# Block sums of the resident operands made in pieces during the up products and kept in DRAM, instead of inside the refill

## The chip, the core and the metric

One core of a Trainium2 chip runs the whole kernel. The metric is the device time of one execution in microseconds; the time of a kernel is the median of several executions. A trace of one more execution was taken by the hardware profiler.

The engines by the profile's names: PE is TensorE (matmuls; PEld its weight loads), DVE is VectorE, ACT is ScalarE, POOL is GpSimd, SP is SyncE, which here only issues DMAs. Each engine works through its own instructions in order and waits on semaphores of the others. So does SP: a DMA whose buffer is not free yet holds up the DMAs behind it.

## The reference

One transformer layer with a mixer of two kinds of groups and a dense SwiGLU FFN, in float32. The change touches only the FFN:

```python
# x: (1, 2048, 1024); w_gate_up: (1024, 5632); w_down: (2816, 1024)
xn = rms_norm(x, ffn_norm_g[l])
gate, up = jnp.split(xn @ w_gate_up[l], 2, axis=-1)
x = x + (jax.nn.silu(gate) * up) @ w_down[l]
return rms_norm(x, final_norm_g)
```

## The kernel before

The attention, the gating and the output projection come first and end at about 1099 us of the trace; what follows is the FFN, and all of the change lies there.

**Products.** Each FFN matrix product is done on 2 x 2 blocks by a scheme with seven products instead of eight (Strassen's, in Winograd's form). One side, the resident operand, stays in SBUF for a whole *set* of work; the other side streams past it. The seven resident operands R0 to R6 come from the four blocks b11, b12, b21, b22 of the resident matrix: R0, R2 and R6 are b11, b21 and b22 as they are, R1, R3, R4 and R5 are sums, made by four adds, each of which builds on the one before: b12 = b22 - b12, b11 = b11 + b12, b21 = b21 - b11, b11 = b22 - b11. Every operand is then split into a high half in fp32r (a cast on ACT) and a low half (a subtraction on DVE), and a product is three matmuls a k-block: high x high, high x low, low x high.

**Sets, groups, rounds.** There are five sets: set 1 and set 2 are the up products (`Up`, 22 items each; the resident matrix is the transposed normed x, tensors XT[0] and XT[1] in DRAM), sets 3 to 5 are the down products (`Down`, 8 items each; the resident matrix is a part of w_down). The list `slots` runs over groups of two items and the seven products n = 0 to 6 of each. I call one n of one group a round: two items x 12 matmuls of 128x128 x 512 columns (9 in set 5). A group is 7 rounds, 168 matmuls (126 in set 5). Set 1 has 11 groups, 77 rounds.

**Streamed operands.** `load` fetches an item's rows (tile raw, or rawd for some down items) by DMAs on SP; `stream` makes its seven operands with four adds, two on POOL and two on DVE (`SE = 'pvpv'`, rows raw<-raw), and `split` gives each a wh (cast on ACT) and a wl (DVE). There are NW = 6 buffers each of wh and wl, and LW = 6 operands are made ahead, which is three rounds. raw has five buffers, so a load waits until an earlier item's split has let go of one.

**Results.** A product lands in one of six PSUM banks (tile pp) and is taken from there by ACT or DVE (`evac`: rows u, c, hT, xa, xb). In the order of the program the bank of a round is written again two rounds after that round at the earliest. The up products' hT is stored to DRAM (HD) and read back by the down products; the down products add to rows of x in the tiles xa, xb and, in the last set, sg.

**The refill, which the change edits.** `staged(s)` loads the four blocks of the next set's resident matrix into four tiles sg0 to sg3 of 128 x 2048 f32 (1 MB each; 128 x 1536 in set 5). The first add is put four rounds into the group ahead of a set's last one. In the last group of a set, `refill` makes the remaining adds and the seven splits (`keep`, `keep_as`), one operand a round, so that each R is replaced behind its last use. Table `TE` names the engine of each add: DVE, but POOL for the third add (b21 = b21 - b11) of set 5 and of set 1, which is never refilled. In the trace the adds are the rows sg<-sg,sg, and the splits' low halves the rows wl<-sg, wh<-sg, R1l, R3l, R4l<-sg (R0, R2, R5 and R6 live in tiles tagged wh and wl).

**What sets the order.** The functions write the work in program order; a scheduler then orders each engine's instructions, by priority and by when it takes operands and buffers to be ready. So an add can come earlier than the place at which it is written: the first add of set 3's sums stands in the first group of set 2.

Of the kernel before, what the change touches and what calls it, by code (L numbers as in the profile page):

```python
# [8 lines left out]
F32 = mybir.dt.float32  # L9
F32R = mybir.dt.float32r  # L10
AF = mybir.ActivationFunctionType
ALU = mybir.AluOpType
# [4 lines left out]
P = 128  # L17
S = 2048
D = 1024
# [6 lines left out]
CH = 512  # L26
# [25 lines left out]
KB = [8, 8, 6]  # L52
# [3 lines left out]
TE = ['vvvv', 'vvpv', 'vvvv', 'vvvv', 'vvvv', 'vvpv']  # L56
# [29 lines left out]
def trunk(ctx: ExitStack, tc: tile.TileContext, x, x_t, mix_g, w_in, b_f, ln_g, ln_b, w_st, b_st, on_g, w_out,  # L86
# [444 lines left out]
    for c in range(NCH):  # L531
# [4 lines left out]
        n = 0  # L536
# [761 lines left out]

    def staged(s):

        sg = stage()
        for i, t in enumerate(sg):
            if s < 3:
                ld(t, XT[s - 1][i])
                continue
            kh, r0 = KB[s - 3] // 2, sum(KB[: s - 3])
            r0 = (r0 + (i // 2) * kh) * P
            ld(t[:, 0:kh, :],
               w_down[r0 : r0 + kh * P, (i % 2) * CH : (i % 2 + 1) * CH].rearrange("(k p) n -> p k n", p=P))
        return sg  # L1310

# [7 lines left out]
    def tt(e, o, a, b, op):  # L1319
        (nc.vector if e == "v" else nc.gpsimd).tensor_tensor(o, a, b, op)  # L1320

    def keep_as(i, src, kh=4):
        rh, rl = resident(i)
        hi_of(nc.scalar, rh[:, 0:kh, :], src)
        lo_of(nc.vector, rl[:, 0:kh, :], src, rh[:, 0:kh, :])
        return rh, rl

    def refill(sg, kh, te):

        b11, b12, b21, b22 = (t[:, 0:kh, :] for t in sg)  # L1330

        def keep(i, src):
            return keep_as(i, src, kh)

        yield keep(0, b11)
        tt(te[1], b11, b11, b12, ALU.add)
        yield keep(1, b11)
        yield keep(2, b21)
        tt(te[2], b21, b21, b11, ALU.subtract)
        tt(te[3], b11, b22, b11, ALU.subtract)  # L1340
        yield keep(3, b11)
        yield keep(4, b12)
        yield keep(5, b21)
        yield keep(6, b22)
# [107 lines left out]
    class Down(Rows):  # L1452
# [15 lines left out]
        def source(self, t):  # L1468
            return XA[t]
# [131 lines left out]
    nextR = [None] * 7  # L1601
    for q in range(len(slots)):
# [7 lines left out]
        if n == 0 and i == 2 and s < 5:  # L1610
            sg = staged(s + 1)
        last = last and s < 5
        if n == 4 and s < 5 and i + 2 * len(its) == len(sets[s - 1]):
            b = [t[:, 0 : sets[s][0].kh, :] for t in sg]
            tt(TE[s + 1][0], b[1], b[3], b[1], ALU.subtract)
        if n == 0 and last:
            fill = refill(sg, sets[s][0].kh, TE[s + 1])
# [75 lines left out]
```

## Time and profile before

| | |
|---|---|
| median of 3 runs | 2384.66 us (2383.82 to 2389.83) |
| the profiled execution | 2382.4 us, span 2380.7 us |
| PE busy in the span | 2337.5 us (98%) |
| DVE, ACT, POOL busy | 1671.2 (70%), 1056.2 (44%), 633.6 us (27%) |
| granted TensorE clock, mean | 0.996 |
| first matmul of sets 1 to 5 | 1099.46, 1521.32, 1942.67, 2100.32, 2253.97 us |
| DMA over the span | 372.22 MB, mean 156 GB/s |

The span is what the profiler saw from the first to the last instruction; the execution's time has 1.7 us around it. A matmul of 512 columns has a row of about 0.39 us, but matmuls overlap in the pipeline; they start one every 0.227 us (38.08 us for the 168 of a group). Where a group takes longer, TensorE stood still or its clock was lower. A row of a list of groups reads: line, engine, operation, output<-inputs, shape, count | busy us, mean ns | idle time of the engine just before, and what ended it.

### The profile page before, as it was taken

To read this page: it belongs to the slowest core of one execution; us is meant where nothing else is said; L and a number is where in the kernel's file an instruction comes from. 1 tells how busy PE (TensorE), PEld (TensorE's weight loads), DVE (VectorE), ACT (ScalarE), POOL (GpSimd) and SP (SyncE) were. 2 spreads that over 40 slices of the span, in tenths; PEclk is the share of its full clock that TensorE was granted. 3 is DMA by queue.
4 is the path that set the end of the run, shared out by engine and by line. 5 is a ranking of instruction groups with operands and counts; after the bars stand their busy time and mean duration, and the time that the engine had idled before them with its cause. 6 is when DMAs were issued, how large, how long until landed. Compare 5 with 4: busy or idle time off the path is not lost. (4 is left out here: it accounts for less than half of the span.)

```text
span 2380.7 us, 31420 instructions
## 1 busy us (share of the span) xinstructions
PE 2337.5 (98%) x10582; PEld 1893.8 (80%) x10582; DVE 1671.2 (70%) x2736; ACT 1056.2 (44%) x1770; POOL 633.6 (27%) x705
## 2 busy tenths in 40 slices
PE   9999999999999989999999999999999999999997
PEld 7778777777777768878888888788888878888886
DVE  6658668888887676566655556965655596686888
ACT  5322137777778776344323233432323242332433
POOL 1100002122111232221323223332322245354531
PEclk9999999999999999999999999999999999999999
DMA  7845567666586664666232332433232345455453
GB/s 257 295 154 195 200 189 209 167 164 178 151 219 190 195 186 150 211 217 200 80 89 81 88 89 80 143 89 96 71 89 72 88 142 186 168 186 200 151 192 148
DMA packets 356425, 372.22 MB, mean 156 GB/s; under 512 B 22101, under 2 KB 275733, under 8 KB 354217
## 3 DMA queue, kind: packets, MB, share of 16 engines
q1 hardware_dynamic: 340280, 326.97, 45.3%
q0 software_dynamic: 7616, 27.33, 3.2%
q10 hardware_dynamic: 8368, 15.91, 1.8%
q8 instruction: 85, 1.39, 0.2%
q14 instruction: 76, 0.61, 0.1%
HBM read 249.15 MB, written 120.98 MB: 155 GB/s over the span
## 5 line engine op out<-in xcount | busy, mean ns | idle before, releaser
L128 ACT CAST wh<-raw 128x512 fp32r<-128x512 f32 (+2 forms) x492 | 301.9, 621 | 746.8 <-PE pp L1631 612.7
L131 DVE TENSOR_TENSOR wl<-raw,wh 128x512 fp32r<-128x512 f32 (+2 forms) x496 | 375.9, 767 | 81.5 <-ACT wh L128 81.0
L1631 PE MATMUL pp<-wl,wh 128*128 128x512 f32 x1056 | 325.3, 389 | 1.2 <-ACT u L1386 1.0
L1631 PE MATMUL pp<-wh,wh 128*128 128x512 f32 x1056 | 325.2, 389 | 0.0
L1320 POOL TENSOR_TENSOR raw<-raw 128x512 f32<-128x512 f32 (+1 forms) x124 | 171.2, 1382 | 518.3 <-DMA raw<-in_w_gu_dram 354.5
L131 DVE TENSOR_TENSOR Pl<-Pt,Ph 128x512 fp32r<-128x512 f32 (+1 forms) x320 | 195.6, 616 | 71.1 <-ACT Ph L128 69.8
L1631 PEld LDWEIGHTS pp<-wl,wh 128*128 128x128 f32 x1056 | 198.0, 188 | 43.0 <-ACT u L1386 1.4
L1631 PEld LDWEIGHTS pp<-wh,wh 128*128 128x128 f32 x1056 | 198.2, 188 | 41.0
L732 ACT ACTIVATE Pt<-mx_ps 128x512 f32<-128x512 f32 (+1 forms) x320 | 169.3, 533 | 122.8 <-PE mx_ps L730 118.4
L1631 PE MATMUL pp<-wl,wl 128*128 128x512 f32 x528 | 205.7, 390 | 1.2 <-DVE wl L131 1.2
L1631 PE MATMUL pp<-wh,wl 128*128 128x512 f32 x528 | 205.4, 389 | 0.0
L887 PE MATMUL z<-wh,xz 128*128 128x512 f32 x496 | 189.0, 396 | 2.0 <-DMA xz<-XS 2.0
L1320 DVE TENSOR_TENSOR raw<-raw,raw 128x512 f32<-128x512 f32 (+1 forms) x112 | 133.9, 1198 | 81.0 <-POOL raw L1320 77.7
L128 ACT CAST Ph<-Pt 128x512 fp32r<-128x512 f32 (+1 forms) x320 | 175.8, 556 | 18.4 <-PE tp L764 4.0
L365 DVE TENSOR_REDUCE mx<-mx_ps 128x1 f32<-128x512 f32 x192 | 130.2, 682 | 28.2 <-PE mx_ps L363 24.3
L742 POOL TENSOR_SCALAR_AFFINE_SELECT Ph<-Ph 128x128 fp32r<-128x128 f32 x128 | 52.3, 408 | 350.4 <-DVE Pl L131 267.2
L363 PE MATMUL mx_ps<-D,A 66*128 66x512 f32 (+2 forms) x320 | 119.6, 376 | 5.1 <-DMA D<-KH 3.6
L762 PE MATMUL tp<-Ph,V 128*128 128x512 f32 (+1 forms) x320 | 118.4, 370 | 5.1 <-POOL Ph L742 3.8
L767 PE MATMUL tp<-Pl,V 128*128 128x512 f32 (+1 forms) x320 | 118.7, 371 | 3.4 <-DVE Pl L131 2.6
L729 PE MATMUL mx_ps<-A,D 74*128 74x512 f32 (+1 forms) x320 | 118.9, 372 | 0.8 <-ACT Pt L732 0.5
L1631 PEld LDWEIGHTS pp<-wl,wl 128*128 128x128 f32 x528 | 99.1, 188 | 22.9 <-DVE wl L131 2.3
L730 PE MATMUL mx_ps<-B,C 128*128 128x512 f32 (+1 forms) x320 | 117.2, 367 | 0.0
(342 smaller groups left out, 5298.4 us busy)
## 6 DMA issues: line engine op xcount, KB each, us to landing
raw<-in_w_gu_dram SPq DMA_DIRECT2D x88, 512.0 KB
xz<-XS SPq DMA_DIRECT2D x31, 1024.0 KB
HD<-hT SPq DMA_DIRECT2D x44, 512.0 KB
D<-KH SPq DMA_DIRECT2D x112, 128.0 KB
XA<-xa SPq DMA_DIRECT2D x27, 512.0 KB
raw<-HD SPq DMA_DIRECT2D x24, 512.0 KB
XA<-xb SPq DMA_DIRECT2D x21, 512.0 KB
xa<-XA SPq DMA_DIRECT2D x20, 512.0 KB
```

What stands on the lines that cost most here:

```text
L128: return nc.scalar.copy(o, i) if eng is nc.scalar else eng.tensor_copy(o, i)
L131: return eng.tensor_tensor(o, i, f(h), ALU.subtract)
L363: last_mx.append(nc.tensor.matmul(pm[:, 0:n], lhs, Dt[0 : lhs.shape[0], 0:n], start=True, stop=True))
L365: nc.vector.tensor_reduce(mx[:, a, s : s + 1], pm, AX.X, ALU.max)
L729: nc.tensor.matmul(st[:, off:], Dt[:, b * P : (b + 1) * P], A[:, off:], start=True, stop=False)
L730: nc.tensor.matmul(st[:, off:], C[:, b * P : (b + 1) * P], B[:, off:], start=False, stop=True)
L732: nc.scalar.activation(Pt[:, off:], st[:, off:], AF.Exp)
L762: nc.tensor.matmul(pv[:, off:], V[:, 0:P], Ph[:, off:], start=kb == 0, stop=False)
L767: nc.tensor.matmul(pv[:, off:], V[:, 0:P], Pl[:, off:], start=False, stop=kb == 4 * j + 3)
L887: nc.tensor.matmul(pz, xz[a][:, k, :], w[b][:, k, :], start=n == 0, stop=n == 3 * KT - 1)
L1320: (nc.vector if e == "v" else nc.gpsimd).tensor_tensor(o, a, b, op)
L1631: nc.tensor.matmul(pm, a[:, k, :], b[:, k, :], start=on is None and k == 0 and e == 0, stop=k == it.kh - 1 and e == 2, skip_group_check=n ...
```

## The change

The sums of the blocks no longer belong to the refill. A generator, `block_sums`, makes them ahead, for sets 2 to 5, in 15 pieces: for each k-block it loads the four 128x512 pieces of b11, b12, b21 and b22 into two xa tiles, makes the four adds on DVE on 128x512, and stores the four results to a DRAM tensor SM of that set. It is advanced by one step in each round from group 1 on (a step is the loads, one add, or the stores). xa has two buffers, and a piece fills both. The refill now only fetches: `fetch` gets operand n either from the matrix itself (n = 0, 2, 6) or from SM (n = 1, 3, 4, 5); four fetches are issued up to four groups ahead of the last group of a set (two for the shorter sets' eight items), the other three in the last group, each into the sg tile of the operand split just before it. So there are seven loads of 1 MB a refill and no add. Table `TE` is gone, and with it the one add of set 5's refill that ran on POOL.

```diff
--- before.py
+++ after.py
@@ -53,7 +53,6 @@
 NF_ = 6
 RL = 2
 SQ = 'p'
-TE = ['vvvv', 'vvpv', 'vvvv', 'vvvv', 'vvvv', 'vvpv']
 SE = 'pvpv'
 NY = 4
 NR = 5
@@ -1296,18 +1295,51 @@
     def stage():
         return [T(pers, [P, 4, CH], F32, f"sg{n}") for n in range(4)]
 
+    def block(s, i):
+
+        if s < 3:
+            return XT[s - 1][i]
+        kh, r0 = KB[s - 3] // 2, sum(KB[: s - 3])
+        r0 = (r0 + (i // 2) * kh) * P
+        return w_down[r0 : r0 + kh * P, (i % 2) * CH : (i % 2 + 1) * CH].rearrange("(k p) n -> p k n", p=P)
+
     def staged(s):
 
         sg = stage()
         for i, t in enumerate(sg):
-            if s < 3:
-                ld(t, XT[s - 1][i])
-                continue
-            kh, r0 = KB[s - 3] // 2, sum(KB[: s - 3])
-            r0 = (r0 + (i // 2) * kh) * P
-            ld(t[:, 0:kh, :],
-               w_down[r0 : r0 + kh * P, (i % 2) * CH : (i % 2 + 1) * CH].rearrange("(k p) n -> p k n", p=P))
+            ld(t, block(s, i))
         return sg
+
+    SM = {s: T(dram, [P, 4, 4, CH], F32, f"SM{s}") for s in (2, 3, 4, 5)}
+
+    def source(s, n):
+
+        if n in (0, 2, 6):
+            return block(s, {0: 0, 2: 2, 6: 3}[n])
+        return SM[s][:, {1: 0, 4: 1, 5: 2, 3: 3}[n], 0 : sets[s - 1][0].kh]
+
+    def fetch(s, n):
+
+        t = T(pers, [P, 4, CH], F32, f"sg{n % 4}")[:, 0 : sets[s - 1][0].kh]
+        ld(t, source(s, n))
+        return t
+
+    def block_sums():
+
+        for s in (2, 3, 4, 5):
+            for k in range(sets[s - 1][0].kh):
+                t = [T(xap, [P, D], F32, "xa") for _ in range(2)]
+                b = [t[i // 2][:, (i % 2) * CH : (i % 2 + 1) * CH] for i in range(4)]
+                for i in range(4):
+                    ld(b[i], block(s, i)[:, k])
+                yield
+                for o, x, y, op in ((1, 3, 1, ALU.subtract), (0, 0, 1, ALU.add), (2, 2, 0, ALU.subtract),
+                                    (3, 3, 0, ALU.subtract)):
+                    tt("v", b[o], b[x], b[y], op)
+                    yield
+                for a in range(2):
+                    ld(SM[s][:, 2 * a : 2 * a + 2, k], t[a].rearrange("p (c n) -> p c n", c=2))
+                yield
 
 
 
@@ -1325,23 +1357,14 @@
         lo_of(nc.vector, rl[:, 0:kh, :], src, rh[:, 0:kh, :])
         return rh, rl
 
-    def refill(sg, kh, te):
-
-        b11, b12, b21, b22 = (t[:, 0:kh, :] for t in sg)
-
-        def keep(i, src):
-            return keep_as(i, src, kh)
-
-        yield keep(0, b11)
-        tt(te[1], b11, b11, b12, ALU.add)
-        yield keep(1, b11)
-        yield keep(2, b21)
-        tt(te[2], b21, b21, b11, ALU.subtract)
-        tt(te[3], b11, b22, b11, ALU.subtract)
-        yield keep(3, b11)
-        yield keep(4, b12)
-        yield keep(5, b21)
-        yield keep(6, b22)
+    def refill(s, sg):
+
+        kh = sets[s - 1][0].kh
+        for n in range(7):
+            r = keep_as(n, sg[n], kh)
+            if n < 3:
+                sg.append(fetch(s, n + 4))
+            yield r
 
     def stream(a11, a12, a21, a22):
 
@@ -1599,6 +1622,7 @@
     make()
     load(1)
     nextR = [None] * 7
+    sums = block_sums()
     for q in range(len(slots)):
         p, n = slots[q]
         s, i, its, last = grp[p]
@@ -1607,14 +1631,13 @@
             if s == 5:
                 finb = T(pers, [P, 4, CH], F32, "sg0")[:, 0:2, :].rearrange("p a n -> p (a n)")
                 ld(finb, fin_g.rearrange("(o n) -> o n", o=1).broadcast_to([P, D]))
-        if n == 0 and i == 2 and s < 5:
-            sg = staged(s + 1)
+        if n == 0 and i == max(2, len(sets[s - 1]) - 8) and s < 5:
+            sg = [fetch(s + 1, m) for m in range(4)]
         last = last and s < 5
-        if n == 4 and s < 5 and i + 2 * len(its) == len(sets[s - 1]):
-            b = [t[:, 0 : sets[s][0].kh, :] for t in sg]
-            tt(TE[s + 1][0], b[1], b[3], b[1], ALU.subtract)
         if n == 0 and last:
-            fill = refill(sg, sets[s][0].kh, TE[s + 1])
+            fill = refill(s + 1, sg)
+        if p:
+            next(sums, None)
         while nq < len(slots) and len(made) + len(grp[slots[nq][0]][2]) <= LW:
             make()
         if n == 0:
```

What it moves, as the built programs show it. In these rows 128x2048 or 128x512 is the output's shape, numbers in names are buffers; L130 in the new kernel is L131 of the old one (a split's low half), L1352 is L1320 (`tt`, every add through it), L1439 and L1472 are the raw loads and the HD stores (L1416, L1449 before), L1334 and L1341 the loads and stores of `block_sums`.

DVE in the last group of set 1, before, from the first sum that is left there to the last; xa, u and c are evacuations and wl<-raw the streamed splits:

```order
L1320 TENSOR_TENSOR sg_3278_12595<-sg_3278_12595,sg_3279_12596 128x2048
L131 TENSOR_TENSOR wl_15214<-raw_3700_15034,wh_15213 128x512
L131 TENSOR_TENSOR wl_15218<-raw_3702_15038,wh_15217 128x512
L131 TENSOR_TENSOR wl_15250<-raw_3701_15036,wh_15249 128x512
L131 TENSOR_TENSOR R1l_15210<-sg_3278_12595,R1h_15209 128x2048
L131 TENSOR_TENSOR wl_15254<-raw_15040,wh_15253 128x512
L1437 TENSOR_TENSOR c_15160<-u_15159,pp_15257 128x512
L131 TENSOR_TENSOR wl_12174<-sg_3280_12597,wl_12174 128x2048
L1437 TENSOR_TENSOR c_15164<-u_15163,pp_15270 128x512
L1320 TENSOR_TENSOR sg_3280_12597<-sg_3280_12597,sg_3278_12595 128x2048
L131 TENSOR_TENSOR wl_15292<-raw_3700_15034,wh_15291 128x512
L1320 TENSOR_TENSOR sg_3278_12595<-sg_3281_12598,sg_3278_12595 128x2048
```

and now, the same stretch:

```order
L130 TENSOR_TENSOR wl_15352<-raw_3726_15164,wh_15351 128x512
L130 TENSOR_TENSOR wl_15356<-raw_3728_15168,wh_15355 128x512
L130 TENSOR_TENSOR R1l_15344<-sg_3585_14365,R1h_15343 128x2048
L130 TENSOR_TENSOR wl_15396<-raw_3727_15166,wh_15395 128x512
L130 TENSOR_TENSOR wl_15400<-raw_15170,wh_15399 128x512
L130 TENSOR_TENSOR wl_12178<-sg_3586_14367,wl_12178 128x2048
L1460 TENSOR_TENSOR c_15292<-u_15291,pp_15403 128x512
L1460 TENSOR_TENSOR c_15296<-u_15295,pp_15416 128x512
L130 TENSOR_TENSOR wl_15437<-raw_3726_15164,wh_15436 128x512
L130 TENSOR_TENSOR wl_15441<-raw_3728_15168,wh_15440 128x512
L130 TENSOR_TENSOR R3l_15432<-sg_3587_14369,R3h_15431 128x2048
```

The three adds sg<-sg,sg of 128x2048 are gone from between the splits; R1, R2 and R3 are split straight from what was fetched.

DVE in the second group of set 1, before, between the splits and the evacuations c and hT of the rounds n = 3 and n = 4:

```order
L131 TENSOR_TENSOR wl_12720<-raw_3227_12297,wh_12719 128x512
L131 TENSOR_TENSOR wl_12724<-raw_3229_12301,wh_12723 128x512
L1437 TENSOR_TENSOR c_12639<-u_12638,pp_12727 128x512
L131 TENSOR_TENSOR wl_12756<-raw_12295,wh_12755 128x512
L1437 TENSOR_TENSOR c_12643<-u_12642,pp_12740 128x512
L131 TENSOR_TENSOR wl_12760<-raw_3228_12299,wh_12759 128x512
L1439 TENSOR_TENSOR c_12639<-c_12639,pp_12763 128x512
L1440 TENSOR_TENSOR hT_12637<-u_12638,pp_12763 128x512
L131 TENSOR_TENSOR wl_12803<-raw_12793,wh_12802 128x512
L1320 TENSOR_TENSOR raw_12793<-raw_12795,raw_12793 128x512
```

and now:

```order
L130 TENSOR_TENSOR wl_12729<-raw_3233_12305,wh_12728 128x512
L1460 TENSOR_TENSOR c_12641<-u_12640,pp_12732 128x512
L130 TENSOR_TENSOR wl_12762<-raw_12299,wh_12761 128x512
L1460 TENSOR_TENSOR c_12645<-u_12644,pp_12745 128x512
L130 TENSOR_TENSOR wl_12766<-raw_3232_12303,wh_12765 128x512
L1352 TENSOR_TENSOR xa_13347<-xa_13348,xa_13347 128x512
L1352 TENSOR_TENSOR xa_13347<-xa_13347 128x512
L1352 TENSOR_TENSOR xa_13348<-xa_13348,xa_13347 128x512
L1462 TENSOR_TENSOR c_12641<-c_12641,pp_12769 128x512
L1463 TENSOR_TENSOR hT_12639<-u_12640,pp_12769 128x512
L130 TENSOR_TENSOR wl_12811<-raw_12801,wh_12810 128x512
L1352 TENSOR_TENSOR xa_13348<-xa_13348,xa_13347 128x512
```

The four adds of one piece (xa<-xa) have come in ahead of the evacuations of round n = 4. All 15 pieces stand like this, from round 3.5 of set 1 (the first) to round 41 (the last).

SP in the same group, before: two stores of the results, then the four loads for the next group, then the next two stores:

```order
L1449 DMA HD_140_203<-hT_12395 128x8x128
L1449 DMA HD_140_203<-hT_12399 128x8x128
L1416 DMA raw_3318_12797<-in_w_gu_dram 128x8x128
L1416 DMA raw_3319_12799<-in_w_gu_dram 128x8x128
L1416 DMA raw_12795<-in_w_gu_dram 128x8x128
L1416 DMA raw_3364_13073<-in_w_gu_dram 128x8x128
L1449 DMA HD_140_203<-hT_12637 128x8x128
L1449 DMA HD_140_203<-hT_12641 128x8x128
```

and now, from the stores of one piece's sums to those of the next:

```order
L1341 DMA SM_2986_11107<-xa_13093 128x2x512
L1341 DMA SM_2986_11107<-xa_13094 128x2x512
L1439 DMA raw_3320_12805<-in_w_gu_dram 128x8x128
L1334 DMA xa_13347<-XT_120_183 128x512
L1334 DMA xa_13347<-XT_121_184 128x512
L1439 DMA raw_3321_12807<-in_w_gu_dram 128x8x128
L1334 DMA xa_13348<-XT_122_185 128x512
L1334 DMA xa_13348<-XT_123_186 128x512
L1439 DMA raw_12803<-in_w_gu_dram 128x8x128
L1439 DMA raw_3370_13099<-in_w_gu_dram 128x8x128
L1341 DMA SM_2986_11107<-xa_13347 128x2x512
L1341 DMA SM_2986_11107<-xa_13348 128x2x512
```

The loads of a piece stand between the raw loads, and the stores of its sums, which wait for DVE's adds, stand ahead of whatever comes next. The two loads xa<-XA of the first down items, which stood at the start of set 1, now come after the last piece's stores, in round 41 to 42.

## Prediction

> **What bounds the kernel now.** I read the page's table of engines first, then the second half of the run cut into groups of products (stages), then the waits of TensorE, then VectorE's own instructions at a change of set.
>
> ```profile
> PE 2337.5 (98%) x10582; PEld 1893.8 (80%) x10582; DVE 1671.2 (70%) x2736; ACT 1056.2 (44%) x1770; POOL 633.6 (27%) x705
> ```
>
> TensorE is the bound: 43 us of 2380.7 are not busy, so nothing that only relieves another engine can gain more than the stalls it ends. The edit touches the five sets of products alone. One window a group shows where time is lost there. Columns: length, then busy time of PE, PEld, DVE, ACT, POOL, granted clock, DMA share, GB/s.
>
> ```profile
> 1178.60:1216.68 38.08, 38.08 (x169) 31.53 (x168) 21.97 (x30) 11.83 (x20) 10.88 (x9) 1.00 0.29 83
> 1483.24:1521.32 38.08, 38.08 (x169) 31.53 (x168) 34.97 (x31) 19.95 (x22) 9.02 (x6) 1.00 0.37 111
> 1521.32:1561.87 40.55, 38.96 (x170) 31.30 (x168) 36.53 (x41) 15.47 (x25) 18.48 (x10) 1.00 0.51 156
> 1904.59:1942.67 38.08, 38.08 (x170) 31.53 (x168) 34.98 (x33) 19.97 (x22) 11.31 (x7) 1.00 0.36 119
> 1942.67:1986.08 43.41, 40.25 (x169) 32.55 (x168) 37.72 (x39) 14.22 (x22) 29.19 (x16) 0.96 0.58 198
> 2062.24:2100.32 38.08, 38.08 (x169) 31.53 (x168) 33.55 (x32) 18.78 (x19) 16.58 (x6) 1.00 0.45 156
> 2100.32:2139.73 39.41, 38.47 (x169) 31.38 (x168) 33.28 (x35) 11.77 (x18) 21.24 (x12) 1.00 0.63 220
> 2215.89:2253.97 38.08, 38.08 (x169) 31.53 (x168) 34.31 (x32) 17.70 (x23) 15.50 (x9) 1.00 0.41 137
> 2253.97:2282.64 28.67, 28.67 (x127) 23.57 (x126) 23.36 (x34) 8.47 (x17) 13.19 (x9) 1.00 0.80 275
> 2282.64:2311.20 28.56, 28.56 (x127) 23.65 (x126) 24.76 (x43) 11.55 (x23) 9.66 (x10) 1.00 0.46 155
> ```
>
> The first row is an undisturbed group of the up products: 168 matmuls in 38.08 us, TensorE never idle, VectorE 58% busy. Below it stand, for each of the four changes of set, the last group of the old set and the first of the new; the last row is an undisturbed group of the fifth set (126 matmuls). Every last group takes exactly 38.08 us; the loss comes in the group after it: 40.55 - 38.08 = 2.47, 43.41 - 38.08 = 5.33, 39.41 - 38.08 = 1.33, and 28.67 - 28.56 = 0.11 us. Together 9.24 us: that is all there is to gain at these places.
>
> ```profile
> PE pp L1631 <- DVE wl L131: 3.8, 4, 2.2
> PE pp L1631 <- ACT u L1386: 1.0, 1, 1.0
> PE pp L1631 <- ACT wh L128: 0.9, 1, 0.9
> ```
>
> These are all of TensorE's waits from 1140 us on (total, times, longest): mostly for a split's low half on VectorE. What VectorE had to do from 1483.24 to 1561.87 us, the last group of set 1 and the first of set 2:
>
> ```profile
> L131 DVE TENSOR_TENSOR wl<-raw,wh 128x512 fp32r<-128x512 f32 x28 | 21.5, 793 | 0.0
> L1320 DVE TENSOR_TENSOR raw<-raw,raw 128x512 f32<-128x512 f32 x8 | 9.7, 1226 | 6.7 <-POOL raw L1320 6.7
> L1320 DVE TENSOR_TENSOR sg<-sg,sg 128x2048 f32<-128x2048 f32 x4 | 9.6, 2405 | 0.0
> L131 DVE TENSOR_TENSOR wl<-sg,wl 128x2048 fp32r<-128x2048 f32 x2 | 5.5, 2758 | 0.0
> L131 DVE TENSOR_TENSOR wh<-sg,wh 128x2048 fp32r<-128x2048 f32 x2 | 5.3, 2647 | 0.9 <-ACT wh L128 0.9
> ```
>
> The four block sums (sg<-sg,sg) cost 9.6 us here, three of them in the last group, one early in the next. In these two groups VectorE is busy 34.97 + 36.53 = 71.5 of 78.63 us (91%); at the second change 89%, at the third 86%, at the fourth 57.7 of 66.75 (86%), where almost nothing is lost. So the loss begins at about 86%.
>
> **Part 1, the sums leave the refill.** Per change, four adds of about 2.4 us leave VectorE (in the last refill one of them leaves POOL). At the first change 71.5 - 9.6 = 61.9 us remain in a length of 76.2 without the stall: 81%, below the 86% at which only 0.11 us is lost. The other changes lose the same adds. I take each to end as the fourth does, with 0.11 us: gain 9.24 - 4 x 0.11 = 8.8 us. What is late next are the seven low halves (2.6 to 2.8 us each by the last two rows), which stay; bounds of this term: nothing, and 9.24 us.
>
> In 5.33 us of it the clock has a part:
>
> ```profile
> 1956.36 0.50 PE L1631 MATMUL pp<-R3h,wl 128*128 128x512 f32 x1 [2.19 <-DVE wl L131]
> 1956.00:1962.00 6.00, 5.64 (x18) 0.72 0.60 191
> ```
>
> After a wait of 2.19 us the granted clock is 0.72 for 6 us, about 0.28 x 6 = 1.7 us of matmul time; it goes with the wait. The Trainium skill's page "TensorE: Matmul & The Clock Gate" (Part 1: The HAM clock gate) has the half clock follow an idle window of about 3.4 us. By that rule a wait of 2.19 us would not bring it, the 1.7 us would have another cause and could stay, and the gain would be 7.1 us; the trace shows it right behind the wait, so I count it.
>
> **Part 2, the sums come into the up products.** 15 pieces (k = 4 + 4 + 4 + 3), each four loads of 256 KB, four adds of 128x512, two stores of 512 KB. The order puts their adds from round 3.5 to round 41 of the products (a round is 24 matmuls, 38.08 / 7 = 5.44 us): 37.7 rounds, 205 us, 13.6 us a piece, 2.8 pieces a group. A 128x512 add of two SBUF tiles:
>
> ```profile
> 1205.26 0.69 DVE L1320 TENSOR_TENSOR raw<-raw,raw 128x512 f32<-128x512 f32 x1
> 1216.85 1.76 DVE L1320 TENSOR_TENSOR raw<-raw,raw 128x512 f32<-128x512 f32 x1 [1.40 <-POOL raw L1320]
> ```
>
> 0.69 us alone, 1.76 where POOL works at the same time. POOL is busy 10.88 of 38.08 us (29%), so I take 0.69 + 0.29 x 1.07 = 1.0 us. A group gets 2.8 x 4 x 1.0 = 11.2 us more: 21.97 + 11.2 = 33.2 of 38.08. That lies beside the products; cost 0, with ends at 29.7 (0.69 each) and 41.7 us (1.76 each, over the group).
>
> The new waits matter more. The adds stand in VectorE's order ahead of evacuations and splits and wait for their loads; the next piece's loads wait on SP for the stores to land, since there are two xa buffers and each piece fills both. What the transfers take, by SP's issues and POOL's wait:
>
> ```profile
> 1116.20 1.21 SPq L1133 DMA_DIRECT2D XT<-xo  x2
> 1118.88 0.33 SPq L1304 DMA_DIRECT2D sg<-XT  x1
> 1119.31 0.39 SPq L1416 DMA_DIRECT2D raw<-in_w_gu_dram  x1
> ...
> 1193.55 8.92 SPq L1416 DMA_DIRECT2D raw<-in_w_gu_dram  x4
> 1197.58 1.29 POOL L1320 TENSOR_TENSOR raw<-raw 128x512 f32<-128x512 f32 x1 [13.22 <-DMA raw<-in_w_gu_dram]
> ...
> SPq L1416 <- DVE wl L131: 107.2, 28, 8.7
> ```
>
> A load that depends on a store goes out at most 2.7 us after the store (1116.20 to 1118.88); two that wait for nothing go out 0.43 us apart (1118.88 to 1119.31); 512 KB land 4.0 us after issue (1193.55 to 1197.58). So four loads land in about 4.0 + 3 x 0.43 = 5.3 us, and a piece's loop is adds 4 x 1.0, store 2.7, loads 5.3: 12.0 us, against 13.6 of room. Some xa loads stand behind raw loads, which go out (8.92 - 0.39) / 3 = 2.8 us apart, since each waits for a split to free its buffer (last row: total, times, longest). So single pieces will come 3 to 6 us late, and VectorE will stand still that long. Who waits: the evacuations behind it, whose banks are written again two rounds later (six banks, 10.9 us), and the splits:
>
> ```profile
> ACT wh L128 <- PE pp L1631: 160.5, 87, 2.1
> ```
>
> From 1140 to 1400 us ACT's casts wait for products to free the six wh buffers, so splits run three rounds, 16.3 us, ahead. A lateness under 10.9 us costs TensorE nothing; I take 0. Ends: 0, and the second rival's price. Raw loads behind a store of sums go out up to 5 us later; the same 16.3 us cover them, and the POOL adds that wait for them. Without that cover each would cost its full lateness.
>
> **Part 3, seven fetches instead of four** in the refill, 1 MB each (0.75 in the last): three more a change. Fetch 4, 5 and 6 wait for splits 0, 1 and 2 to free their buffer and are needed four rounds (21.8 us) later; by the raw load's 4.0 us for 512 KB, 1 MB lands in under 8. SP stands at them with raw loads queued behind, about 3 us late, inside the 16.3. DMA share in these windows is 0.36 to 0.63. Cost 0; ends 0 and 3 us. The two xa<-XA loads of the down products move behind the pieces and still go out in round 42 of set 1's 77 rounds, for a set that starts at 1942.67: 0.
>
> **Sum.** -8.8 + 0 + 0. The profiled execution took 2382.4 us (span 2380.7 and 1.7 around it) and would take 2373.6; it lies 2.3 under the median 2384.66, so on the scale of the runs 2375.9: 2376 us, -0.37%. A difference under 0.3% (7.15 us) is about what a measurement of this kernel can't tell from no change.
>
> **Rivals.** (B) Partly: the change to the down products keeps its loss, because POOL (29.19 of 43.41 us) and the first down operands, not the sums, make it late. For it: that group has POOL's highest load, and one wait there is for ACT's u. Against: the long wait ended with VectorE's split. Gain 8.8 - 5.2 = 3.6: 2381 us, no change that can be told.
> (C) The other side: the piece's loop is longer than its room, and VectorE, in order, is paced by it. From 12.0 us it needs only 4.0 more, by transfers that share the engines with raw loads: at 16 us a piece, 15 x (16 - 13.6) = 36 us late, less 10.9 of cover, 25 lost: 2376 + 25 = 2401. It ends slower by over 0.3% from a loop of about 15.4 us on. For it: one chain of store, load and add with no spare buffer. Against: the sum of its parts.
> (D) Every new add meets POOL at 1.76 us: 41.7 us a group, 3.6 over, in 205 / 38.08 = 5.4 groups 19.4 late, less 10.9: 8.5 lost, 2384.4, the same. Against it: POOL's 29%. The Trainium skill's "GPSIMD Engine Reference" (8. Key points) says that GpSimd contends with VectorE instructions that have two SBUF inputs, which all 60 adds have and the old sums had too; the two rows of 0.69 and 1.76 us agree.
> That the sums stay in the refill is ruled out by the order: no sg<-sg,sg stands there any more.
>
> **How the numbers follow.** Forecast 0.60 (0.53 beyond 0.3%, 0.07 just inside), B 0.20, D 0.07, C 0.10, the rest 0.03 on either side. Faster 0.53, same 0.35, slower 0.12. The range goes down to 2372: all 9.24 us gone give 2375.4, and the first group of set 1,
>
> ```profile
> 1099.46:1140.52 41.06, 40.37 (x185) 33.04 (x184) 33.61 (x39) 18.62 (x28) 9.60 (x7) 1.00 0.63 206
> ```
>
> is 2.98 us over the 38.08 and loses two of its four sg<-XT loads to a later place, so it may gain up to that. It goes up to 2388, which takes in B, D and a loop a little over its room; C is left out.
>
> **What would show it.** Right: the first groups of sets 2 to 4 at 38.1 to 38.3 us, the clock 1.00 there, VectorE near 28 us in the last groups and near 33 in the first six, all of them still 38.08 long. Wrong: groups 1 to 6 of set 1 over 38.08 with VectorE's xa adds idle before them, waiting for DMA (C); adds near 1.76 (D); 43 us at the start of set 3 (B).

## The result: 1% slower, and where the time went

The median of five runs is 2412.03 us (2405.02 to 2413.07), against 2384.66 us before: a ratio of 1.0105, 95% interval 1.0094 to 1.0117. The forecast was 2376 us.

The profiled execution took 2412.1 us, 29.7 more than the one of before. Three parts make it up. The first matmul of the FFN comes at 1107.39 us instead of 1099.46, 7.9 us later, though the order of instructions up to there is the same but for one load on SP; the last experiments show that this does not belong to the change. What lies behind the last matmul is 1.2 us shorter. The rest, 23.0 us, is in the FFN, and three stages of the changed kernel show its sign in each: set 1, set 2, and sets 3 to 5. Columns as in the table by group above (length, then busy time of PE, PEld, DVE, ACT, POOL, granted clock, DMA share, GB/s):

```profile
1107.39:1558.59 451.20, 430.64 (x1865) 352.49 (x1864) 307.97 (x399) 143.50 (x231) 123.75 (x88) 0.98 0.56 172
1558.59:1977.47 418.88, 418.88 (x1850) 346.85 (x1848) 261.32 (x338) 142.48 (x227) 123.31 (x88) 1.00 0.34 101
1977.47:2399.46 421.99, 419.62 (x1849) 346.61 (x1847) 320.07 (x419) 148.13 (x236) 163.10 (x115) 1.00 0.54 190
```

The same three stages of the kernel before:

```profile
1099.46:1521.32 421.86, 421.17 (x1865) 348.35 (x1864) 268.42 (x340) 145.14 (x230) 119.41 (x86) 1.00 0.34 99
1521.32:1942.67 421.35, 419.76 (x1850) 346.61 (x1848) 269.94 (x344) 141.83 (x227) 129.32 (x89) 1.00 0.32 94
1942.67:2368.50 425.83, 421.73 (x1849) 347.40 (x1847) 331.65 (x426) 147.43 (x237) 186.01 (x118) 1.00 0.51 177
```

Set 1, in which the pieces are made, is 29.3 us longer; set 2 is 2.5 and sets 3 to 5 are 3.8 us shorter. So the refill did gain, 6.3 us, and the pieces took nearly five times that. By group, the changed kernel's set 1 from its second group to its seventh, an undisturbed one behind the pieces, and then the first groups of sets 2 to 5:

```profile
1148.45:1188.00 39.55, 38.39 (x169) 31.46 (x168) 24.93 (x34) 9.65 (x17) 10.27 (x8) 1.00 0.66 199
1188.00:1233.23 45.23, 41.54 (x169) 33.48 (x168) 33.57 (x48) 12.83 (x23) 11.55 (x9) 0.92 0.77 244
1233.23:1272.82 39.59, 38.39 (x170) 31.45 (x168) 28.39 (x39) 10.50 (x19) 9.56 (x7) 1.00 0.68 210
1272.82:1320.16 47.34, 40.32 (x169) 32.20 (x168) 32.05 (x42) 11.40 (x20) 13.98 (x10) 0.93 0.66 206
1320.16:1366.70 46.54, 40.92 (x170) 33.28 (x168) 29.93 (x43) 11.40 (x20) 11.19 (x8) 0.93 0.60 189
1366.70:1406.27 39.57, 38.38 (x169) 31.45 (x168) 27.94 (x39) 13.30 (x23) 15.56 (x11) 1.00 0.44 133
1406.27:1444.35 38.08, 38.08 (x169) 31.53 (x168) 21.93 (x30) 11.84 (x20) 10.89 (x9) 1.00 0.29 83
...
1558.59:1596.67 38.08, 38.08 (x169) 31.53 (x168) 31.11 (x37) 15.24 (x24) 15.44 (x9) 1.00 0.49 139
...
1977.47:2018.50 41.03, 38.66 (x169) 31.38 (x168) 34.58 (x37) 13.57 (x21) 22.92 (x14) 1.00 0.54 185
...
2132.74:2170.82 38.08, 38.08 (x169) 31.54 (x168) 32.66 (x35) 12.31 (x19) 17.38 (x12) 1.00 0.67 237
...
2285.06:2313.62 28.56, 28.56 (x127) 23.66 (x126) 22.58 (x34) 8.97 (x17) 12.84 (x11) 1.00 0.70 258
```

In the six long groups VectorE is busy 25 to 34 us of 39 to 47: it is not overloaded, it stands. What it and the others stand for, from 1130 to 1376 us (the pieces), in the changed kernel's waits by engine (total, times, longest):

```profile
DVE xa L1352 <- DMA xa<-in_w_down_dram: 31.6, 7, 7.0
DVE raw L1352 <- POOL raw L1352: 20.1, 13, 3.6
DVE xa L1352 <- DMA xa<-XT: 14.4, 3, 7.7
...
SPq L1341 <- DVE xa L1352: 109.1, 28, 10.3
SPq L1472 <- POOL hT L1470: 29.3, 10, 5.9
...
ACT hT L1469 <- DVE u L1468: 48.2, 11, 7.3
...
PE pp L1654 <- ACT u L1454: 17.4, 5, 5.7
```

Read from the bottom: TensorE waits for ACT to take a product out of its bank (u); ACT, in order, waits for VectorE's u; VectorE waits 46 us for the loads of the pieces (xa); SP, which has to issue those loads, waits for VectorE's adds, since the stores of the piece before stand ahead of them, and for POOL's hT, since stores of results stand among them. That is one loop.

### The profile page after: what moved, and what is told of

It is laid out like the page before. It is cut to its first block, busy times and chain, and to the rows that moved or that the text cites. A ratio compares the mean times of both kernels' runs of the same rounds, so it can differ in the third digit from the quotient of the medians.

```text
span 2410.4 us, 31687 instructions
## 1 busy us (share of the span) xinstructions
PE 2348.3 (97%) x10582; PEld 1901.6 (79%) x10582; DVE 1689.5 (70%) x2781; ACT 1056.5 (44%) x1770; POOL 609.2 (25%) x704
## 5 line engine op out<-in xcount | busy, mean ns | idle before, releaser
L130 DVE TENSOR_TENSOR wl<-raw,wh 128x512 fp32r<-128x512 f32 (+2 forms) x496 | 374.1, 764 | 64.1 <-ACT wh L127 63.6
L1654 PE MATMUL pp<-wl,wh 128*128 128x512 f32 x1056 | 331.3, 395 | 19.8 <-ACT u L1454 18.8
L1352 POOL TENSOR_TENSOR raw<-raw 128x512 f32<-128x512 f32 (+1 forms) x124 | 170.4, 1376 | 551.0 <-DMA raw<-in_w_gu_dram 351.7
L130 DVE TENSOR_TENSOR Pl<-Pt,Ph 128x512 fp32r<-128x512 f32 (+1 forms) x320 | 195.5, 616 | 72.9 <-ACT Ph L127 71.5
L1352 DVE TENSOR_TENSOR raw<-raw,raw 128x512 f32<-128x512 f32 (+1 forms) x112 | 133.9, 1197 | 77.7 <-POOL raw L1352 74.2
```

Of the source, the lines that this page charges most:

```text
L130: return eng.tensor_tensor(o, i, f(h), ALU.subtract)
L1654: nc.tensor.matmul(pm, a[:, k, :], b[:, k, :], start=on is None and k == 0 and e == 0, stop=k == it.kh - 1 and e == 2, skip_group_check=n ...
```

## Experiments

All lengths below are taken from the FFN's own groups, from first to last matmul, so that the chance at its start does not enter. "Lost in set 1" is what groups 2 to 11 take beyond 38.08 us each, in one profiled execution of each kernel; the changed kernel's second one lost 31.0 us, so differences under about 2 us between two losses say nothing. Each ratio goes against executions of the kernel before from the same session (medians 2384.66 to 2386.22 us) and is worked out from all executions, so it is not the quotient of the two medians.

| kernel | lost in set 1 | FFN, us | time, median | ratio to before (95%) |
|---|---|---|---|---|
| before | 0 | 1269.0 | 2384.66 | |
| changed | 29.3 | 1292.1 | 2412.03 | 1.0105 (1.0094 to 1.0117) |
| no sums | 0 | 1263.0 | 2379.48 | 0.9976 (0.9961 to 0.9991) |
| spread | 0 | 1263.8 | 2378.45 | 0.9974 (0.9965 to 0.9983) |
| dense, four buffers | 0.9 | 1263.8 | 2379.25 | 0.9976 (0.9967 to 0.9984) |
| dense, no loads | 0 | 1263.0 | 2380.29 | 0.9976 (0.9967 to 0.9985) |
| held, 2.5 rounds | 13.5 | 1276.5 | 2393.3 | 1.0029 (1.0018 to 1.0041) |
| held, two loads | 12.7 | 1275.4 | 2391.01 | 1.0018 (1.0010 to 1.0027) |
| held, 3 rounds | 6.8 | 1269.5 | 2384.84 | 0.9991 (0.9982 to 1.0000) |
| held, four buffers | 6.6 | 1269.5 | 2386.29 | 1.0002 (0.9993 to 1.0010) |
| spread, adds on VectorE | 0 | 1262.4 | 2379.56 | 0.9970 (0.9959 to 0.9981) |

### What the refill alone gains

No pieces, and a block in the place of each sum:

```diff
-        return SM[s][:, {1: 0, 4: 1, 5: 2, 3: 3}[n], 0 : sets[s - 1][0].kh]
+        return block(s, {1: 1, 4: 1, 5: 2, 3: 3}[n])
...
-        if p:
-            next(sums, None)
```

> The changed kernel with the pieces left out altogether: no piece is loaded, added or stored, and the refill fetches a block of the matrix in the place of each sum (the sums are left out; the fetches, their sizes and the splits stay). Every theory: groups 2 to 7 of set 1 go back to 38.08 us, and the first groups of sets 2 to 5 read 38.08, about 41, 38.08 and 28.56 us as in the changed kernel, 6.3 us less than before. Time 2378 us if the 7.9 us by which the changed kernel's FFN began late (1107.4 against 1099.5 us) were chance or belong to the pieces' buffers in DRAM; 2386 if they belong to the fetches or to the longer program.

Set 1 went back to 38.08 us in every group, and the first groups of sets 2 to 5 took 38.08, 41.30, 38.08 and 28.56 us. The FFN is 1263.0 us, 6.0 less than before; that is the whole gain of the refill, and the seven fetches cost nothing that shows. At set 3 something stays that the sums did not make:

```profile
1945.65:1986.95 41.30, 38.67 (x169) 31.38 (x168) 34.49 (x37) 13.56 (x21) 23.47 (x15) 1.00 0.53 187
```

### Spread over six rounds

In the changed kernel the pieces are written one step a round, six rounds a piece, but the scheduler put them 2.6 rounds apart, by my reading wherever its own times said that the loads had landed. Here loads and adds are queued behind an instruction of the round in which they are written (`behind`: later in the same engine's order, with no wait for its end):

```diff
+    def held(e):
+        return behind(anchor[e]) if e in anchor else ExitStack()
...
-                for i in range(4):
-                    ld(b[i], block(s, i)[:, k])
+            with held("s"):
+                for i in range(4):
+                    ld(b[i], block(s, i)[:, k])
...
+            with held("v"):
                 tt("v", b[o], b[x], b[y], op)
```

Here `anchor["s"]` is the last raw load or HD store written, `anchor["v"]` VectorE's last evacuation. The loads of piece j (counted from 0) are written at round 7 + 6 j, the adds two to five rounds later, the stores one round after the last add.

> The changed kernel with each piece's loads and adds held behind the rounds at which they are written, so that a piece takes six rounds (32.6 us) instead of 2.6 (14.3 us): same work, same two buffers. Theory L (the loop of store, loads and adds takes 16.7 us in a place of 14.3, and VectorE is paced by it): with 32.6 us of room the 29.3 us lost in groups 2 to 7 of set 1 vanish, less than 2 us are left, 2378 to 2380 us where the FFN starts as before, 2386 to 2388 where it starts 7.9 us late. Theory W (the work itself, 60 adds and 45 MB of transfers beside the raw loads, costs its time wherever it stands): 15 to 29 us stay, spread over 15 groups.

No group of set 1 behind the first is over 38.08 us (the third group stands below); 0.7 us is lost in set 2. Interval between pieces 32.6 us, as written, and the adds hardly wait for loads (4.9 + 2.4 us over 15 pieces). Time 2378.45 us: the same sums, made in the same two buffers, cost 0.8 us of FFN against the kernel without them. This does not yet tell the loop from the work, since the density has changed too.

```profile
1180.30:1218.38 38.08, 38.08 (x169) 31.53 (x168) 24.44 (x34) 11.83 (x20) 11.28 (x9) 1.00 0.47 139
```

### As dense, with the loads ahead

The pieces in the four sg tiles, which lie idle then, one piece in each:

```diff
-                t = [T(xap, [P, D], F32, "xa") for _ in range(2)]
+            u = T(pers, [P, 4, CH], F32, f"sg{j % 4}")
```

They are held as in the spread kernel: the loads of piece j at round 7 + 2.5 j, the adds four to 5.5 rounds later, the stores half a round after.

> The changed kernel with the pieces as dense as there (2.5 rounds each), but in the four sg tiles, one piece in each, with the loads issued four rounds ahead of the adds: same adds, loads and stores in about the same groups, the loop opened by buffers. Theory L: at most 5 us of the 29.3 us are left, 2378 to 2383 us where the FFN starts as before (7.9 more where it starts late). Theory W: 20 us or more stay, 2398 us and up.

0.9 us lost. VectorE is as busy as in the long groups and DMA as full, with no loss, here the counterpart of 1188.00 and of 1272.82 us above:

```profile
1180.93:1219.01 38.08, 38.08 (x169) 31.53 (x168) 31.46 (x43) 11.51 (x20) 11.73 (x8) 1.00 0.78 240
...
1257.09:1295.17 38.08, 38.08 (x169) 31.53 (x168) 31.45 (x43) 12.18 (x21) 13.01 (x9) 1.00 0.71 225
```

So neither the 60 adds nor the bytes are what costs. No VectorE add waits for a load of its piece here.

### As dense, without the loads

> The changed kernel with the pieces as dense as there, but only the first piece is loaded; the others add and store the same two buffers over again (the later pieces' loads are left out, so their sums are not those of the blocks). VectorE has the same 60 adds, the stores stay, 52 of the 60 loads of 256 KB twice over are gone: the loop is adds and stores alone, about 5.5 + 2.5 = 8 us by the changed kernel's trace. Theory L: under 3 us of the 29.3 are left. Theory W in the form that VectorE's adds cost the time: 20 us or more stay; in the form that the loads' traffic does: they vanish here and not in the kernel with four buffers.

The generator's loads run for the first piece alone (`if j: return`); 56 of the 60 loads are gone, not 52 as the expectation says. The pieces' first adds came 13.5 us apart, closer than in the changed kernel, and set 1 lost nothing at all; its fourth group:

```profile
1222.52:1260.60 38.08, 38.08 (x170) 31.53 (x169) 29.99 (x42) 11.14 (x20) 12.26 (x8) 1.00 0.48 152
```

Adds and stores cost nothing as long as no add waits for a load. Together with the kernel before this one, that rules theory W out. Both kernels hold the pieces behind other instructions, though, as the changed kernel does not; whether the holding is the cure is what the next kernel asks.

### How long the loop is: three kernels with held pieces

The three that follow take spread's code, with the four adds of a piece a quarter of a round apart and the pieces closer: the loads of piece j at round 7 + 2.6 j and the adds 1.1 rounds later, or, in the last of the three, at round 7 + 3 j and 1.5 rounds later.

> A control for the kernels that hold the pieces: the changed kernel's pieces with two xa buffers and four loads, held so that their first adds stand 2.52 rounds (13.7 us) apart in VectorE's order, 35.2 rounds from the first to the last piece. Theory L: the loop of 16.4 us is 2.7 longer than its room, 14 x 2.7 = 38 us, less about two rounds (10.9 us) of lateness that the evacuations stand: 27 us lost in set 1 (20 to 32), 2405 us. If instead the holding had cured the spread kernel: under 5 us.

13.5 us lost, half of the forecast 27: a miss in size. Its worst group:

```profile
1261.66:1306.85 45.19, 40.80 (x170) 33.22 (x168) 29.66 (x40) 11.40 (x20) 13.71 (x10) 0.92 0.62 196
```

So holding alone is no cure: with two buffers and 13.7 us of room the loss is there. The pieces' first adds came 15.2 us apart, not 16.4. In its waits and in the changed kernel's the difference is on SP: here no store of results stands among the four loads, which are issued within 3.0 us on average, against 5.2 in the changed kernel. That this is what makes the other half of the loss is a reading of the two traces; no run changes it alone.

> The same as the control, with the same order of all adds, but in the 11 pieces of the down sets each xa tile is filled by one load of 512 KB in the place of two of 256 KB: same bytes, same adds, two DMAs fewer to get through SP's queue in each loop. Theory L1 (the loop is long because its four loads are issued 5.2 us from first to last, behind other DMAs of SP and their waits): the loop falls by 2.5 to 3.5 us to about 13.5, which fits its room, and the loss falls from 27 to under 8 us. Theory L2 (the loads are slow because of their bytes): the loop stays over 16 us and the loss over 20 us.

```diff
-                    ld(b[i], block(s, i)[:, k])
...
+                    for a in range(2):
+                        r0 = (sum(KB[: s - 3]) + a * (KB[s - 3] // 2) + k) * P
+                        ld(u[a], w_down[r0 : r0 + P])
```

(u is the piece's two xa tiles; the four pieces from XT keep their four loads.)

12.7 us lost, 15.2 us a piece: no different from the control. Theory L1 fell, and L2's loop of over 16 us was not seen either. In the 11 pieces with two DMAs fewer the issues became 0.5 us shorter (3.1 to 2.6 us), and the wait from the last issue to the first add 0.3 us longer (4.9 to 5.2).

> The control with the pieces' adds 3.0 rounds (16.3 us) apart instead of 2.52, nothing else. Theory L: loop and room are equal, what lateness there is stays under the two rounds: at most 2 us lost in set 1, 2379 to 2381 us. Theory W (each of the 15 pieces costs its time in work): two thirds of the control's loss or more stay, 18 us and up.

The lead of the loads grew here too (1.1 to 1.5 rounds), so the expectation's "nothing else" is not so. 6.8 us lost where 2 were expected, 5.3 of them in one group:

```profile
1255.53:1298.87 43.34, 39.96 (x170) 32.65 (x169) 31.47 (x42) 11.30 (x20) 15.62 (x11) 0.96 0.62 197
```

The interval grew to 17.2 us with the room (16.3). So the loop has no fixed length of 16.4 us, as I had it: it is what it was given plus what each piece comes late, since between its four adds stand other instructions of VectorE, with waits of their own. Theory W's 18 us did not come.

### Buffers, or the lead of the loads?

The control in the four sg tiles, with loads still written 1.1 rounds ahead:

> The control with held pieces (first adds about 2.5 rounds apart, the loads written 1.1 rounds ahead of them), but in the four sg tiles in the place of the two xa tiles: a piece's loads need not wait for the stores of the piece before, yet they are not asked for earlier as in the dense kernel with four buffers (there four rounds ahead). The control lost 13.5 us in set 1, at 15.2 us a piece against 13.7 of room; the dense one lost 0.9. If the buffers close the loop (a load can't go out until the store before it has landed), under 4 us are left here, about 2380 us. If it is the short lead (loads 1.1 rounds, 6 us, ahead of adds that need them 5 us after the last is issued), 8 to 13 us are left, 2386 to 2391 us.

6.6 us, between the two. The waits of VectorE in it, from 1145 to 1400 us:

```profile
DVE raw L1387 <- POOL raw L1387: 38.7, 21, 4.7
...
DVE sg L1387 <- DMA sg<-in_w_down_dram: 15.2, 4, 5.0
DVE sg L1387 <- DMA sg<-XT: 7.3, 2, 5.1
```

Of the control's 13.5 us, buffers alone take away half; 5.7 of the other 6.6 go in the dense kernel with four buffers, whose loads lead by four rounds (its adds also stand half a round apart instead of a quarter, so the lead is the likely cause and not the only difference). The first row tells of a second way in which a late add may cost. SP stands at the piece's store until the adds are done, the raw loads behind it go out late, POOL's adds on them too, and VectorE waits for POOL: 38.7 us here, 34.8 in the control, 27.1 in the dense kernel with four buffers, 21.5 in the changed kernel and 19.6 in the one before, over the same stretch. In SP's timeline of this kernel:

```profile
1244.34 0.38 SPq L1361 DMA_DIRECT2D SM<-sg  x1
1244.95 4.75 SPq L1474 DMA_DIRECT2D raw<-in_w_gu_dram  x3
1249.79 1.65 SPq L1361 DMA_DIRECT2D SM<-sg  x1
1251.54 0.42 SPq L1474 DMA_DIRECT2D raw<-in_w_gu_dram  x1
```

Three raw loads go out behind the first store, the last one behind the second, at 1251.54. VectorE stands 3.8 us for POOL until 1254.73, for an add that had waited for the second of the three, and 2.1 us until 1259.36, for one that had waited for the last. How much of the changed kernel's 29.3 us goes by this way and how much by the adds' own waits, no run here separates; both begin with an add that waits for its load, for without the loads nothing was lost.

### What stays at set 3

The spread kernel, with the stream adds of the first two down items all on VectorE:

```diff
-            self.ops = stream(*self.raw)
+            self.ops = stream(*self.raw, SE="vvvv" if self.kb == 0 and self.tp < 2 else SE)
```

> The spread kernel (six rounds a piece), and the four stream adds of the first two down items all on VectorE in the place of two on POOL. The first group of set 3 takes 41.3 us there. If POOL's work beside VectorE is what is left of that loss (128x512 adds at 1.77 and a 128x2048 split at 3.38 us while POOL works, against 0.69 and 2.3 to 2.6 alone), it falls to under 39 us, and the time to about 2376 us. If VectorE's own load is what is left, two adds more make it worse: over 42 us.

```profile
1939.90:1980.19 40.29, 38.79 (x169) 31.30 (x168) 32.31 (x39) 13.54 (x21) 19.65 (x13) 1.00 0.60 198
```

Between the two: 41.32 became 40.29 us (one execution; in the ten others with the fetches the group took 41.00 to 41.32 us), so POOL's adds were about 1.0 of the 3.2 us there, and VectorE is busy less in that group (34.5 to 32.3 us) with two instructions more. What keeps the other 2.2 us is open. The FFN is the shortest of all, 1262.4 us; the median does not tell it from the spread kernel.

### The changed kernel and the one before, once more

> The changed kernel once more. In the profiled executions so far the FFN begins at 1099.5 us (before), 1107.4 (changed) and 1098.7 to 1105.3 (the seven variants and the control), with the same order of instructions up to there. If that is chance, it begins anywhere between 1098 and 1107 here, the loss in set 1 is 29 us again within 1 us, and the time is 2405 to 2413 us; if it belongs to the changed kernel, it begins at 1107 again.

> The kernel before once more, one look. By chance alone the FFN begins between 1098 and 1107 us; from there to its last matmul it takes 1269.0 us again, with the first groups of sets 2 to 5 at 40.55, 43.41, 39.41 and 28.67 us.

The FFN of the changed kernel began at 1102.55 us this time and the one before at 1102.46: the 7.9 us do not belong to the change. Set 1 lost 31.0 us (29.3 the first time, so a miss of the 1 us that I allowed), the FFN took 1294.0, and the median was 2408.93 us, ratio 1.0093 (1.0079 to 1.0106). The FFN before took 1269.9 us, with 41.17, 43.47, 39.44 and 28.68 us in the first groups.

## Why the prediction was wrong, point by point

**The step that failed** is the piece's loop in part 2: 12.0 us against 13.6 of room. The lateness that was to stay under its cover was not, and part 2's 0 became 29.3 us. Rival C, to which I gave 0.10, is what happened, at nearly its price (16 us a piece, 25 lost), though not mainly for the reason it gave, slower transfers: from the last load's issue to the first add the measured time is only 0.5 us over mine (table below). From the first add of one piece to that of the next the changed kernel took 16.4 us on average, and the order gives (39.88 - 3.54) rounds x 5.44 / 14 = 14.1 us of room (13.6 in the prediction, which divided by 15). The loop by its parts, averaged over 14 pieces:

| part of the loop | taken as | measured, us |
|---|---|---|
| store issued to first load issued | 2.7 | 1.5 |
| first to last of four load issues | 1.3 | 5.2 |
| last load to first add | 4.0 | 4.5 |
| the four adds of the piece before | 4.0 | 5.1 |

The loads were the largest error: I spaced them 0.43 us apart, as DMAs that wait for nothing. In the trace the second pair often waits until the second of the stores before has landed (SP's waits: 11.8 us in 11 times), since each xa tile comes free with its own store, and in some pieces other DMAs stand among the loads. In three of the 14 these are stores of results, and there the four issues take 8.7 to 8.8 us; in the other eleven they take 4.3 on average (2.7 to 6.9). SP's timeline for one of the three, and VectorE's first add behind it:

```profile
1281.15 4.01 SPq L1341 DMA_DIRECT2D SM<-xa  x2
1285.20 1.35 SPq L1334 DMA_DIRECT2D xa<-in_w_down_dram  x2
1288.54 0.38 SPq L1472 DMA_DIRECT2D HD<-hT  x1
1289.02 0.53 SPq L1334 DMA_DIRECT2D xa<-in_w_down_dram  x1
1292.88 0.38 SPq L1472 DMA_DIRECT2D HD<-hT  x1
1293.31 0.57 SPq L1334 DMA_DIRECT2D xa<-in_w_down_dram  x1
```

```profile
1297.45 0.69 DVE L1352 TENSOR_TENSOR xa<-xa,xa 128x512 f32<-128x512 f32 x1 [2.85 <-issue]
```

From 1285.20 to 1293.88 for four loads, because two stores of hT waited for POOL, which waited, by way of ACT, for VectorE, which was late by this loop. I had the raw loads' spacing of 2.8 us in a quoted row and used it only for single late pieces; in the sum it would have given 4.0 + 3 x 2.8 = 12.4 us for the loads and a loop of 19, on the losing side. The adds' part was long less by their duration (3.4 us for four) than by the splits, evacuations and waits that stand between them. No run takes the loop's parts one by one: shown by experiment is that the loss goes when the adds need not wait for their loads, and the shares above are read from one trace. The Trainium skill's page "DMA: Bandwidth & Descriptors" (Anatomy of one DMA) says that a wait on a semaphore happens on the issuing sequencer ahead of the DMA, never in the DMA engines; SP's 109 us of standing at the pieces' stores agree.

**The room was no room.** The program's text has six rounds a piece; the scheduler made 2.6 of them, by my reading because it put each piece where its own times let it be ready. Then the order's 14.1 us a piece were its forecast of the loop, with nothing to spare, and I compared one forecast with another. No run shows the scheduler's times. Spread's 32.6 us, which the program's text has, cost nothing.

**The cover of 10.9 us was right.** The round that TensorE had reached at the first add of pieces 1, 2, 3, 4, 8, 10 and 15 was 0.5, 1.0, 1.8, 2.0, 1.8, 2.3 and 1.3 ahead of the round at which the order has that add: lateness grew to about two rounds, 11 us, and no further, TensorE paying what was added. In the held control it grew to 1.9, in the dense kernel with four buffers to 0.5. The bookkeeping closes, which shows that the readings fit together and not what caused them: 14 x (16.4 - 14.1) = 32 us, less the growth of lateness from 3.0 to 7.2 us, is 28, and 1.5 come after the last piece. For the control 14 x (15.2 - 13.7) - 7.9 = 13, for held 3 rounds 14 x (17.2 - 16.3) - 5.9 = 7.

**The 16.3 us of cover for raw loads were not a cover beside the other.** VectorE's adds on raw stand in the same queue as its evacuations, so a late raw load and a late piece add up within the same 10.9 us. This follows from the order; no run makes raw loads alone late.

**Rival D was wrong, and the work was sized right.** The adds took 0.69 us in the median, and 8 of 60 over 1.5:

```profile
L1352 DVE TENSOR_TENSOR xa<-xa,xa x45: 676/691/1787, 1132.6 to 1369.8; 128x512 f32<-128x512 f32 x45
```

(duration in ns least, median and longest; first and last start). VectorE's 31.5 us a group, in the dense kernel with four buffers, were forecast at 33.2.

**Part 1 was right in kind and large by 2.5 us.** Gain 6.3 of 8.8: three of four changes went to 38.08 or 28.56 us as forecast, and 2.4 rather than 5.2 us went at set 3, where rival B was half right (POOL, about 1.0 us of what stays). The VectorE busy time of last and first group at set 2 fell from 71.5 to 64.2 us, not to 61.9: the other adds and the streamed splits became 3.3 us longer in sum. The border of "about 86%" for VectorE was none: in the prediction's own rows the third change lost 1.33 us and the fourth 0.11, both at 86%, and in the changed kernel the third stood at 87% and lost nothing, the second at 85% and lost 2.95.

**The clock went with the wait, as forecast.** In the first group of set 3 the granted clock is 1.00 now. But in set 1 the same effect came back larger: of the 29.3 us about 22 are TensorE standing (19.9 us in its rows at seven waits, and about 0.3 us more at each: a group with one wait of 1.16 us is 1.47 us longer) and about 7 the clock. The clock was at half in three stretches of 6.83 us (windows cut to them; TensorE's busy time is the second number):

```profile
1202.29:1209.12 6.83, 6.08 (x14) 4.84 (x15) 5.67 (x9) 3.83 (x8) 2.56 (x2) 0.50 0.68 223
1287.62:1294.45 6.83, 3.02 (x7) 2.44 (x8) 5.45 (x6) 3.77 (x7) 3.41 (x3) 0.50 0.70 211
1335.41:1342.23 6.82, 5.41 (x13) 4.24 (x14) 4.41 (x6) 3.82 (x8) 2.51 (x2) 0.50 0.63 179
```

In (6.08 + 3.02 + 5.41) = 14.5 us at half clock 7.3 us of matmul time are lost.

**Part 3, the fetches at nothing, was right:** no sums has all seven and lost nothing by them.

**The change with the pieces held back** comes near what the prediction described: 2378.45 us, ratio 0.9974 (0.9965 to 0.9983). It is faster than the changed kernel and, by a little less than the 0.3% that I had set as a limit, than the one before.

## What to carry to other kernels

Where a load, some work on an in-order engine and a store share buffers, work out the loop from the longest rows of every queue that it passes, other users of that queue included, and compare it with the spacing in the order; a spacing that a scheduler chose by its own estimate may have no slack. Waits that stand in one engine's order share one cover, so add them before comparing with it. If such work is not urgent, hold it to the pace at which it is needed, and issue its loads some rounds ahead; here that turned +1% into -0.26% (six rounds a piece, loads two rounds ahead).

## What the runs showed of the hardware

TensorE's granted clock goes by how long TensorE stood inside windows of 3.41 us, not by the length of a wait. In all thirteen traces the clock changes recorded between 300 us and the end of the FFN fall on a fixed grid of 3.41 us, and each stretch of half clock in the FFN is one or two windows long. The held kernel with two loads has two waits of nearly the same length:

```profile
1234.00 0.72 PE L1694 MATMUL pp<-wl,wh 128*128 128x512 f32 x2 [1.96 <-ACT u L1494]
1358.70 0.73 PE L1694 MATMUL pp<-wl,wh 128*128 128x512 f32 x2 [2.02 <-ACT u L1494]
```

The grid's windows around them (length, TensorE's busy time, and so on; the granted clock stands third from the end):

```profile
1232.05:1235.46 3.41, 1.46 (x6) 1.24 (x7) 2.03 (x3) 3.14 (x6) 2.52 (x2) 1.00 0.93 294
1235.46:1238.87 3.41, 3.41 (x9) 2.67 (x8) 2.86 (x5) 1.64 (x4) 0.00 (x0) 0.50 0.77 224
...
1354.93:1358.34 3.41, 1.75 (x8) 1.13 (x6) 2.60 (x3) 1.31 (x3) 1.58 (x2) 1.00 0.81 260
1358.34:1361.75 3.41, 3.05 (x13) 2.55 (x14) 2.84 (x3) 2.68 (x6) 1.79 (x2) 1.00 0.28 80
```

The first wait lies in one window, TensorE stands 1.95 us of it, and the next window runs at half clock. The second wait, though longer, is split between two windows, 1.66 us in the first, and the clock stays. Over the FFN of all the traces, every window at full clock in which TensorE stood 1.93 us or more was followed by half clock, and none in which it stood 1.67 us or less; nothing lies between. The Trainium skill's page "TensorE: Matmul & The Clock Gate" (Part 1: The HAM clock gate) has the half clock follow an idle window of about 3.4 us; the length agrees with the 3.41 us here, but the window need not be idle all through. One window at half clock costs up to 1.7 us of matmul time beside the wait, two up to 3.4, and less where TensorE stands in them anyway. So the prediction's rival reading of the 2.19 us wait, that the low clock has another cause, does not hold.

The stretch ahead of the FFN, with the same order of instructions in every kernel but for one load, ended anywhere between 1098.7 and 1107.4 us in thirteen profiled executions. Part of that may be the same grid: the clock stood at half for 6.8 to 20.5 us in it, 6.8 where it ended earliest and 20.5 where it ended latest, though no run tests it. For an edit worth 6 us, the length of the edited stage in the trace told more than the medians did.
